# A state-space layer's gate moved from TensorE to VectorE, with the conditioning row turned on chip and one product tile placed in another PSUM bank

## The chip, the cores and the metric

The kernel runs on one core of a Trainium2 chip. The metric is device time in microseconds (us) of one execution, the median of several runs. The engines of the core run their own instruction streams side by side: TensorE (PE: matmuls, and PEld for its weight loads), VectorE (DVE), ScalarE (ACT), GpSimd (POOL), and SyncE (SP), which in this program issues nearly all DMA transfers. Each engine takes its instructions in order, and an instruction that waits for a semaphore holds back all that stands behind it on that engine.

## The reference

The program is a decoder trunk of two layers over 512 tokens of width 1024, float32 throughout. Each layer has a token mixer and a gated feed-forward part with a short convolution; the first layer's mixer is a state-space model (S5), the second's is attention with forgetting. Every one of the four sub-layers is modulated by the conditioning vector c:

```
mod = silu(c) @ ada_w + ada_b
shift, scale, gate = split(mod, 3)
hn = rmsnorm(h) * (1 + scale) + shift
h = h + gate * mixer(hn)
```

The S5 mixer, which is where this case plays, is

```
u = hn @ w_in
y = gelu(state_space(u) + d_skip * u)
y = y * sigmoid(y @ w_glu)
return y @ w_out
```

So for sub-layer 0 three vectors of 1024 numbers are needed from c: shift and scale before u, and the gate only after `y @ w_out`. The next sub-layer (number 1, the feed-forward part) needs its own shift and scale right after that.

## The kernel before, in words

Activations lie with the 1024 channels on the partitions (8 tiles of 128) and the 512 tokens along the free axis. A large product is made tile by tile of 128 output channels. Its weights are split into a rounded part `w_hi` (ScalarE, L280) and the rest `w_lo` (VectorE, L281), its input likewise, and each tile is 8 x 3 matmuls of 128 x 512 into one PSUM bank (`mms`, L297): hi by hi, hi by lo, lo by hi, for each k. A loaded tile of weights is `raw` (L189, 512 KB). There are three buffers for `raw`, five each for `w_hi` and `w_lo`. The eight PSUM banks are two pools of four, `mm` and `aux`.

The stretch around the change runs like this.

1. **Start.** SP loads a first small pack, x, a second pack, and stores `silu(c)` (tile `sc`, 128 x 8) as one row of 1024 numbers in DRAM (`c_row`, L234). It then loads the weights for scale and shift of sub-layer 0 (`in_ada_w`, eight tiles each). TensorE multiplies them (L218) in steps of two tiles, the norm's statistics are made beside it, the columns of 128 numbers are formed by small matmuls (L161, L166) and stored as `ga` and `par` (L171, L174).
2. **S5 loop**, m = 0 to 7. Each turn makes one tile of u (L1169), the group's tables (L957, L973, L980), a scan (L1012, L1023 to L1044), the outputs (L1054, L1062, L1068) and sends y through DRAM. Between these, TensorE does further steps of L218: four for the gate of sub-layer 0 in turns 0 and 1, whose columns follow in turn 1, and eight for shift and scale of sub-layer 1 in turns 2 to 7, the last two turns with two each. The columns of the latter come at the end of the loop.
3. **The head of y @ w_glu.** Four of its eight tiles (HEAD = 4) are accumulated during the loop's end (L1198) in all four banks of `mm`.
4. **The rest of y @ w_glu.** The function `glu` takes a finished tile through a sigmoid (L1256), multiplies it by y (L1257, y read again from DRAM as `yt`) and splits it into `zhi` (L280) and `zlo` (L281). Tiles 4 to 7 are made by `product`, each into a bank of `mm` (L297), so the first of them waits for the sigmoid of tile 0. The residual x is loaded again as `h` (L138) before this.
5. **y @ w_out**, tiles 0 to 7, with `h + gate * tile` on VectorE (L364), followed by the next norm.

In the feed-forward part after it, 56 columns of later shift, scale and gate vectors are made on VectorE instead. One such unit (L248, L249) is a DMA of 128 transposed weight rows (`ada_rows`, 512 KB) and one VectorE instruction that multiplies them by c, broadcast over the partitions (`ada_c`, L240, read from `c_row`), and sums along the row.

Most of the order is set by the framework: it keeps a list in program order, moves instructions ahead by the priorities of its own scheduler, and fixes each engine's order before the run. A stretch at the start is in the order in which it is written (`manual_schedule`). A tile pool that reuses memory makes the new tile wait for the last use of the old.

Of the kernel before, what the change touches and what calls it, by code (L numbers as in the profile page):

```python
# [17 lines left out]
P = 128  # L18
# [28 lines left out]
ROWS_FROM = 1  # L47
# [15 lines left out]
class Trunk:  # L63
# [167 lines left out]
    def spread_c(self):  # L231

        self.cd = self.dram.tile([1, D], F32, name="c_row")
        self.nc.sync.dma_start(self.cd.rearrange("o (k p) -> p (o k)", p=P), self.sc)  # L234

    def ada_pool(self, pool, bufs):

        self.bgpool, self.ada_bufs = pool, bufs
        self.crow = pool.tile([P, D], F32, name="ada_c")
        self.nc.sync.dma_start(self.crow, self.cd.to_broadcast([P, D]))  # L240
# [60 lines left out]
    def product(self, w, ms, nk, x, evac, head=0, tail=0, after=None, ticks=0, halves=HALVES, tail_pool=(), first=None, step=None, apart=False):  # L301
# [17 lines left out]
        for m in ms[head:len(ms) - tail]:  # L319
            wk = self.weights(w[m], nk)  # L320
            ps = self.mm.tile([P, S], F32, name="mmp")
            for c in HALVES if apart else (full,):
                for k in range(nk):
                    self.mms(ps[:, c], wk, x, k, nk, c)
                    if step:
                        step()
            evac(m, ps, full)
            self.tick(ticks)
# [456 lines left out]
class S5(Trunk):  # L785
# [285 lines left out]
    def s5_read_y(self, pool, m):  # L1071
        nc = self.nc
        t = pool.tile([P, L, B], F32, name="yt", bufs=2)
        nc.sync.dma_start(t, self.yd[m].rearrange("g c i b -> (g c) i b"))
        return t[:, ::-1, :]

    def s5(self, i, nxt):
# [5 lines left out]
        with ExitStack() as stack:  # L1083
# [3 lines left out]
            with ExitStack() as start:  # L1087
# [12 lines left out]
                with tc.manual_schedule(engines={ENG.PE, ENG.Activation, ENG.DVE, ENG.SP}):  # L1100
                    self.load_x(self.act)
                    self.load_rest()
                    self.spread_c()
# [52 lines left out]
                    nc.scalar.activation(first, ps.rearrange("p (b j) -> p j b", j=L), AF.Identity, bias=shifted)  # L1156
                    for k in range(2, KT):
                        nc.scalar.activation(x[:, k], x[:, k], AF.Identity, bias=self.par[i][:, k:k + 1])
# [18 lines left out]

            yhi = ylo = None
# [23 lines left out]
            ada = [self.ada_pe(i, (2,), late=True), self.ada_pe(i + 1, (0, 1), late=True)]  # L1202
# [4 lines left out]
            for m in range(KT):  # L1207
                if m:
                    outputs(m - 1)
                with self.behind(*behind):  # L1210
# [6 lines left out]
                    for _ in range((2, 2, 1, 1, 1, 1, 2, 2)[m]):  # L1217
                        next(ada[m >= 2])
                    if m == 1:
                        next(ada[0])  # L1220
# [26 lines left out]
            next(ada[1])  # L1247
        self.load_x(self.ctx.enter_context(tc.tile_pool(name="resid", bufs=1, reuse_waits="tile")))
        with tc.tile_pool(name="s5b", bufs=1, reuse_waits="tile") as pool:
            self.gap(pool, 32, "z_gap")  # L1250
            zhi = pool.tile([P, KT, S], F32R, name="zhi")
            zlo = pool.tile([P, KT, S], F32R, name="zlo")

            def glu(m, ps, cols):
                t = self.tmp.tile([P, S], F32, name="nm_t")
                nc.scalar.activation(t, ps, AF.Sigmoid)  # L1256
                nc.vector.tensor_tensor(tok(t), tok(t), self.s5_read_y(pool, m), ALU.mult)  # L1257
                self.put_parts(zhi[:, m], zlo[:, m], t)

            for m in range(HEAD):  # L1260
                glu(m, gps[m], slice(0, S))
            self.product(self.io["s5_w_glu"], range(HEAD, KT), KT, (yhi, ylo), glu)
            after, y = nxt
            self.product(self.io["s5_w_out"], range(KT), KT, (zhi, zlo), self.add_residual(i), tail=2, after=after)
# [245 lines left out]
def lay_out(inp):  # L1510
# [14 lines left out]
    o["ada_rows"] = np.moveaxis(o["ada_w"][1:], 1, 2).reshape(3, 24, P, D)  # L1525
# [64 lines left out]
```

## Time and profile before

| what | value |
|---|---|
| median of 3 runs | 1240.31 us (1239.1 to 1240.43) |
| the profiled execution, its own time | 1243.44 us |
| its span, first to last instruction | 1241.4 us |
| PE busy | 1213.7 us, 98% |
| PE weight loads busy | 1018.6 us, 82% |
| DVE busy | 899.3 us, 72% |
| ACT busy | 560.5 us, 45% |
| HBM read | 175.57 MB, 147 GB/s over the span |
| S5 loop, in this execution | from about 45 to 204.6 us |
| rest of y @ w_glu | 206.45 to about 228 us |

A busy PE in this profile is not a PE at its peak, since the ends of matmuls are modelled. How long a piece of matmul work takes is better read from the distance of its starts. Times inside a row are counted from the start of the span. A row of the timeline has start, length, engine, line, operation, the tiles written and read, their shape, and a count where several alike are merged; in brackets stands how long the engine was idle before it and what ended that. A row of a window has for each engine its busy time, then the granted TensorE clock (1.00 is full), the busy share of the DMA engines and the GB/s they moved.

### The profile page before, as it was taken

The page shows a single profiled execution, that of the slowest core. Times are in us where ns is not written, and L with a number is a line of the kernel's source. Part 1 is how long each engine was busy: PE and PEld are TensorE (multiplying, and loading weights), DVE is VectorE, ACT ScalarE, POOL GpSimd, SP SyncE. Part 2 cuts the span into 40 slices and gives each one's busy share as a digit, 9 for nine tenths or more (in the row PEclk, how much of TensorE's full clock was granted, in tenths as well). Part 3 has the DMA queues.
Part 4 walks back from the last instruction along what each step waited for, and adds up shares of the span by engine and source line. Part 5 has one row for each costly group of instructions (what it writes and reads, how often), then busy time and mean ns, then how long its engine had stood idle before and what let it go on. Part 6 is the DMA issues. An engine that isn't in the chain of part 4 may idle for free.

```text
span 1241.4 us, 19480 instructions
## 1 busy us (share of the span) xinstructions
PE 1213.7 (98%) x7506; PEld 1018.6 (82%) x7506; DVE 899.3 (72%) x1666; ACT 560.5 (45%) x1031; POOL 56.5 (5%) x109
## 2 busy tenths in 40 slices
PE   6999999999999999999999999999989999999997
PEld 2466678898888788888899888888989999999987
DVE  6898796559887774443567467775799988888865
ACT  3453464334332223333434467654456555555543
POOL 0000000000000000000000134331000000000000
PEclk9899999999999999999999999999999999999999
DMA  9686667326877773222413343330313332333331
GB/s 268 253 275 222 202 196 266 129 100 204 292 267 236 256 248 111 102 75 77 139 69 102 129 142 128 104 130 21 118 52 111 107 117 89 118 105 104 102 86 68
DMA packets 74251, 183.75 MB, mean 148 GB/s; under 512 B 24135, under 2 KB 26527, under 8 KB 73135
## 3 DMA queue, kind: packets, MB, share of 16 engines
q1 hardware_dynamic: 73871, 181.99, 45.2%
q8 instruction: 59, 0.97, 0.3%
q10 hardware_dynamic: 288, 0.52, 0.1%
q14 instruction: 33, 0.27, 0.1%
HBM read 175.57 MB, written 6.92 MB: 147 GB/s over the span
## 4 chain that ended last, share of the span: by engine, by line
PE 83%; DMA 7%; DVE 5%; issue 2%; ACT 1%; POOL 0%; SPq 0%; DVEq 0%; POOLq 0%; ACTq 0%
PE mmp L297 47%; PE mmp L552 10%; DMA ada_raw<-in_ada_rows 5%; PE mmp L1169 5%; PE aux L552 4%; PE mmp L1334 3%; PE aux L973 2%; PE mmp L1198 2%; PE aux L1477 2%; PE mmp L218 1%; PE aux L1460 1%; DVE ada_raw L249 1%; PE aux L1062 1%; PE aux L1054 1%; DVE w_lo L281 1%
## 5 line engine op out<-in xcount | busy, mean ns | idle before, releaser
L280 ACT ACTIVATE w_hi<-raw 128x1024 fp32r<-128x1024 f32 (+4 forms) x197 | 181.2, 927 | 238.8 <-PE mmp L297 150.3
L281 DVE TENSOR_TENSOR w_lo<-raw,w_hi 128x1024 fp32r<-128x1024 f32 (+4 forms) x197 | 210.8, 1071 | 92.5 <-ACT w_hi L280 84.9
L297 PE MATMUL mmp<-a_hi,w_hi 128*128 128x512 f32 (+1 forms) x664 | 242.8, 367 | 2.0 <-ACT a_hi L434 1.3
L297 PE MATMUL mmp<-a_hi,w_lo 128*128 128x512 f32 (+1 forms) x664 | 240.0, 362 | 3.1 <-DVE w_lo L281 3.1
L297 PE MATMUL mmp<-a_lo,w_hi 128*128 128x512 f32 (+1 forms) x664 | 239.7, 362 | 0.0
L297 PE MATMUL mmp<-ghi,w_hi 128*128 128x512 f32 (+1 forms) x394 | 145.2, 369 | 2.1 <-ACT ghi L280 2.1
L297 PE MATMUL mmp<-glo,w_hi 128*128 128x512 f32 (+1 forms) x394 | 145.0, 368 | 0.1
L297 PE MATMUL mmp<-ghi,w_lo 128*128 128x512 f32 (+1 forms) x394 | 144.6, 367 | 0.0
L297 PEld LDWEIGHTS mmp<-a_hi,w_lo 128*128 128x128 f32 x664 | 125.5, 189 | 22.9 <-DVE w_lo L281 3.3
L297 PEld LDWEIGHTS mmp<-a_hi,w_hi 128*128 128x128 f32 x664 | 125.4, 189 | 22.6 <-issue 2.6
L297 PEld LDWEIGHTS mmp<-a_lo,w_hi 128*128 128x128 f32 x664 | 125.7, 189 | 17.5
L249 DVE CUSTOM_DVE_ANT_0 ada_raw<-ada_raw,ada_c,rest 128x1024 f32<-128x1024 f32 x56 | 71.7, 1282 | 29.0 <-DMA ada_raw<-in_ada_rows 28.9
L297 PEld LDWEIGHTS mmp<-ghi,w_hi 128*128 128x128 f32 x394 | 74.3, 189 | 14.3 <-ACT ghi L280 2.6
L297 PEld LDWEIGHTS mmp<-ghi,w_lo 128*128 128x128 f32 x394 | 74.4, 189 | 12.2
L297 PEld LDWEIGHTS mmp<-glo,w_hi 128*128 128x128 f32 x394 | 74.4, 189 | 12.1 <-DVE glo L281 0.5
L364 DVE SCALAR_TENSOR_TENSOR h<-mmp,par,h 128x512 f32<-128x512 f32 (+1 forms) x74 | 49.8, 676 | 42.9 <-PE mmp L297 42.9
L614 ACT ACTIVATE conv<-conv 128x512 f32<-128x512 f32 x44 | 27.6, 631 | 78.5 <-DVE conv L611 78.1
L552 PE MATMUL mmp<-w_lo,w_hi 128*128 128x256 f32 x216 | 59.7, 277 | 0.0
L552 PE MATMUL mmp<-w_hi,w_lo 128*128 128x256 f32 x216 | 59.7, 277 | 0.0
L552 PE MATMUL mmp<-w_hi 128*128 128x256 f32 x216 | 59.7, 277 | 0.0
L1169 PE MATMUL mmp<-a_x,raw 128*128 128x512 f32 x112 | 57.8, 655 | 0.0
L281 DVE TENSOR_TENSOR w_lo<-sums,w_hi 128x1024 fp32r<-128x1024 f32 x40 | 48.5, 1222 | 3.4 <-ACT w_hi L280 2.1
(302 smaller groups left out, 2459.9 us busy)
## 6 DMA issues: line engine op xcount, KB each, us to landing
raw<-in_w_up SPq DMA_DIRECT2D x88, 512.0 KB, 3.3
ada_raw<-in_ada_rows SPq DMA_DIRECT2D x56, 512.0 KB, 4.5
raw<-in_ada_w SPq DMA_DIRECT2D x40, 512.0 KB, 6.4
raw<-in_w_down SPq DMA_DIRECT2D x32, 384.0 KB, 3.1
raw<-in_w_down SPq DMA_DIRECT2D x32, 320.0 KB, 3.0
nf<-nfd SPq DMA_DIRECT2D x8, 1152.0 KB, 5.7
raw<-in_fox_qk SPq DMA_DIRECT2D x16, 512.0 KB, 3.6
h<-in_x SPq DMA_DIRECT2D x8, 512.0 KB, 4.8
```

The lines of the kernel that those rows point to most:

```text
L249: nc.vector.tensor_tensor_reduce(w, w, self.crow, 1.0, self.ada_b[:, i, m:m + 1], ALU.mult, ALU.add, self.par[i][:, m:m + 1])
L280: nc.scalar.activation(hi, src, AF.Copy)
L281: nc.vector.tensor_tensor(lo, src, hi.bitcast(F32), ALU.subtract)
L297: self.last_mm = self.nc.tensor.matmul(o, wt, xt[:, cols], start=(k == 0 and n == 0), stop=(k == nk - 1 and n == 2),)
L364: self.nc.vector.scalar_tensor_tensor(self.h[:, m, cols], ps, self.par[i][:, 16 + m:17 + m], self.h[:, m, cols], op0=ALU.mult, op1=ALU.add,)
L552: self.last_mm = nc.tensor.matmul(o, wt[:, k], xt[:, k], start=(first and k == 0 and n == 0), stop=(k == H - 1 and n == 2), skip_group_che ...
L614: nc.scalar.activation(t, t, AF.Silu)
L973: nc.tensor.matmul(ps[g2][:, j, cols], x[rows, a + j, r].rearrange("p c j -> p (c j)"), self.rr[rows, planes, q, :], start=(j == 0 and r = ...
L1169: nc.tensor.matmul(ps, w[m][:, k, :], x[:, k], start=(k == 0), stop=(k == KT - 1))
L1198: nc.tensor.matmul(gps[m], wt, xt[:, k], start=(k == 0 and part == 0 and xt is yhi), stop=(k == KT - 1 and part == 1))
L1334: self.last_mm = nc.tensor.matmul(ps[q, b][:, :n], xt[:, k, tb], wt, start=(k == 0 and i == 0), stop=(k == KT - 1 and i == 2),)
L1477: nc.tensor.matmul(pv[:, c * P:], self.v[:, hp, k, r].rearrange("p t d -> p (t d)"), pp[:, r, c + 3 * k:NB + 3 * k, :].rearrange("p b t -> ...
```

## The change

It has three parts.

- **The gate of sub-layer 0** is no longer made by TensorE in the S5 loop. It is eight units on VectorE (DMA of `ada_rows` and a row sum each), called by `product` while tiles 5 to 7 of `y @ w_glu` are made, three after a tile (`ticks=3`), with four buffers, and the broadcast of c for them is loaded there too. The steps for shift and scale of sub-layer 1 now come one per turn, m = 0 to 7.
- **The row of c** is turned by TensorE (a transpose to 8 x 128), copied by ScalarE and stored as eight runs of 128 numbers. This stands behind the first tile of u, no longer at the start.
- **Tile 4 of y @ w_glu** goes to a bank of `aux`, its weights are loaded and split ahead of the loop's end, and its matmuls stand ahead of the sigmoids of tiles 0 to 3. Six buffers hold y for the multiplication, where there were two, and the residual is loaded after the product in program order.

```diff
-ROWS_FROM = 1
+ROWS_FROM = 0
...
-        self.cd = self.dram.tile([1, D], F32, name="c_row")
-        self.nc.sync.dma_start(self.cd.rearrange("o (k p) -> p (o k)", p=P), self.sc)
+        nc = self.nc
+        self.cd = self.dram.tile([KT, P], F32, name="c_row")
+        ps = self.aux.tile([KT, P], F32, name="aux")
+        nc.tensor.transpose(ps, self.sc, self.ident)
+        rows = self.tmp.tile([P, S], F32, name="c_rows", tag="ssq", bufs=1)[:KT, :P]
+        nc.scalar.activation(rows, ps, AF.Copy)
+        nc.sync.dma_start(self.cd, rows)
...
-            wk = self.weights(w[m], nk)
-            ps = self.mm.tile([P, S], F32, name="mmp")
+            wk = ready[m] if m in ready else self.weights(w[m], nk)
+            ps = self.aux.tile([P, S], F32, name="aux") if m in ready else self.mm.tile([P, S], F32, name="mmp")
...
-                    self.spread_c()
...
+                    self.spread_c()
                     for k in range(2, KT):
                         nc.scalar.activation(x[:, k], x[:, k], AF.Identity, bias=self.par[i][:, k:k + 1])
...
+            ada = self.ada_pe(i + 1, (0, 1), late=True)
...
-            ada = [self.ada_pe(i, (2,), late=True), self.ada_pe(i + 1, (0, 1), late=True)]
...
-                    for _ in range((2, 2, 1, 1, 1, 1, 2, 2)[m]):
-                        next(ada[m >= 2])
-                    if m == 1:
-                        next(ada[0])
+                    next(ada)
...
-            next(ada[1])
-        self.load_x(self.ctx.enter_context(tc.tile_pool(name="resid", bufs=1, reuse_waits="tile")))
+            next(ada)
+        resid = self.ctx.enter_context(tc.tile_pool(name="resid", bufs=1, reuse_waits="tile"))
...
+            ready = {HEAD: self.weights(self.io["s5_w_glu"][HEAD], KT)}
...
-                nc.vector.tensor_tensor(tok(t), tok(t), self.s5_read_y(pool, m), ALU.mult)
+                nc.vector.tensor_tensor(tok(t), tok(t), self.s5_read_y(pool, m, 6), ALU.mult)
...
-            for m in range(HEAD):
+            self.product(
+                self.io["s5_w_glu"], range(HEAD, HEAD + 1), KT, (yhi, ylo), lambda m, ps, cols: gps.update({m: ps}),
+                ready=ready,
+            )
+            for m in range(HEAD + 1):
                 glu(m, gps[m], slice(0, S))
-            self.product(self.io["s5_w_glu"], range(HEAD, KT), KT, (yhi, ylo), glu)
+            self.ada_pool(pool, 4)
+            self.bg = [self.ada_units(i, [2])]
+            self.product(self.io["s5_w_glu"], range(HEAD + 1, KT), KT, (yhi, ylo), glu, ticks=3)
+            self.load_x(resid)
+            self.done()
...
-    o["ada_rows"] = np.moveaxis(o["ada_w"][1:], 1, 2).reshape(3, 24, P, D)
+    o["ada_rows"] = np.moveaxis(o["ada_w"][0:], 1, 2).reshape(4, 24, P, D)
```

The instruction order shows three places on which the prediction rests. From `y @ w_out` on, the order is the same on every engine.

The first is SP's queue at the start of the program. Before:

```order
L108 DMA first<-in_first 128x168
L138 DMA h<-in_x 128x2x512 x4
L108 DMA rest<-in_rest 128x416
L234 DMA c_row<-sc 128x8x1
L189 DMA raw<-in_ada_w 128x1024 x10
```

And now, up to the store of the row:

```order
L108 DMA first<-in_first 128x168
L138 DMA h<-in_x 128x2x512 x4
L108 DMA rest<-in_rest 128x416
L189 DMA raw<-in_ada_w 128x1024 x10
L189 DMA raw<-in_s_w_in 128x1024
L189 DMA raw<-in_ada_w 128x1024 x6
L800 DMA s_b<-in_s_b 128x1024
L189 DMA raw<-in_s_w_in 128x1024
L1146 DMA s_rr<-in_s_c 128x1024
L1147 DMA s_z<-s_zero 7x8x128
L970 DMA dd<-in_s_dd 128x128
L189 DMA raw<-in_s_w_in 128x1024
```

The row's store (`L239 DMA c_row<-c_rows 8x128`) is the next one. The first weight loads stand directly behind the second pack.

The second is TensorE at the end of the S5 loop, from the last lo products of the head on. Before, with the columns of sub-layer 1 (L161, L166) ahead of tile 4 (L297):

```order
L1198 MATMUL mmp<-a_hi,w_lo 128x512 x4
L161 MATMUL aux<-rest 128x16
L166 MATMUL aux<-sel,ada_rows 128x4 x4
L297 MATMUL mmp<-a_hi,w_hi 128x512
L297 MATMUL mmp<-a_lo,w_hi 128x512
```

Now those columns stand further up, ahead of the last scan's output product (L1067):

```order
L1067 MATMUL aux<-ua,w_1596 128x63 x16
L1204 MATMUL mmp<-a_hi,w_hi 128x512
L1204 MATMUL mmp<-a_lo,w_hi 128x512
L1059 MATMUL aux<-u,t 128x64 x8
L161 MATMUL aux<-rest 128x16
L166 MATMUL aux<-sel,ada_rows 128x4 x4
```

Tile 4 (`L302 MATMUL aux<-a_hi,w_hi 128x512`) follows the last `L1204 MATMUL mmp<-a_hi,w_lo 128x512 x4` directly, in a bank of `aux`.

The third is VectorE during the rest of `y @ w_glu`. Before, from the multiplication of tile 2 and 3 on (`nm_t<-nm_t,yt`), with the weight rests of later tiles (`w_lo`) between:

```order
L1257 TENSOR_TENSOR nm_t<-nm_t,yt 128x8x64 x2
L281 TENSOR_TENSOR w_lo<-raw,w_hi 128x1024
L281 TENSOR_TENSOR zlo<-nm_t,zhi 128x512 x2
L1257 TENSOR_TENSOR nm_t<-nm_t,yt 128x8x64
L281 TENSOR_TENSOR zlo<-nm_t,zhi 128x512
```

Now the same stretch has row sums (`ISA ada_raw`, each followed by a short read of its sum, `ISA par_92`) in between; it is shown from the weight rest of tile 6 up to that of tile 7:

```order
L286 TENSOR_TENSOR w_lo<-raw,w_hi 128x1024
L286 TENSOR_TENSOR zlo<-nm_t,zhi 128x512 x2
L254 ISA ada_raw,par_92<-ada_raw,ada_c,rest 128x1024
L254 ISA par_92 128x1
L1260 TENSOR_TENSOR nm_t<-nm_t,yt 128x8x64 x2
L254 ISA ada_raw,par_92<-ada_raw,ada_c,rest 128x1024
L254 ISA par_92 128x1
L286 TENSOR_TENSOR zlo<-nm_t,zhi 128x512 x2
L254 ISA ada_raw,par_92<-ada_raw,ada_c,rest 128x1024
L254 ISA par_92 128x1
L286 TENSOR_TENSOR w_lo<-raw,w_hi 128x1024
```

Between the weight rest of tile 5 and this stretch stand three more row sums, the multiplications of tiles 0 to 3 and the rests `zlo` of tiles 0 and 1. So six row sums, six multiplications and six `zlo` stand ahead of the weight rest of tile 7, which before stood ahead of the multiplications of tiles 2 and 3.

More of the change, by code (lines that the diff above doesn't have):

```diff
@@ L239, in ada_pool @@
         self.crow = pool.tile([P, D], F32, name="ada_c")
-        self.nc.sync.dma_start(self.crow, self.cd.to_broadcast([P, D]))
+        self.nc.sync.dma_start(self.crow, self.cd.rearrange("k p -> (k p)")[None].to_broadcast([P, D]))
     def ada_units(self, i, thirds):
@@ L299, in mms, with product @@
             )
-    def product(self, w, ms, nk, x, evac, head=0, tail=0, after=None, ticks=0, halves=HALVES, tail_pool=(), first=None, step=None, apart=False):
+    def product(self, w, ms, nk, x, evac, head=0, tail=0, after=None, ticks=0, halves=HALVES, tail_pool=(), first=None, step=None, apart=False, ready=()):
         ms = list(ms)
@@ L1069, in s5_outputs, with s5_read_y @@
         nc.sync.dma_start(self.yd[m].rearrange("g c i b -> (c i) g b"), yg)
-    def s5_read_y(self, pool, m):
+    def s5_read_y(self, pool, m, bufs=2):
         nc = self.nc
-        t = pool.tile([P, L, B], F32, name="yt", bufs=2)
+        t = pool.tile([P, L, B], F32, name="yt", bufs=bufs)
         nc.sync.dma_start(t, self.yd[m].rearrange("g c i b -> (g c) i b"))
```

## The prediction

> **What bounds the kernel now.** I read the page's chain of waits first, then windows of the stretch up to 230 us, its timeline engine by engine, and the groups of the gate product.
>
> ```profile
> PE 83%; DMA 7%; DVE 5%; issue 2%; ACT 1%; POOL 0%; SPq 0%; DVEq 0%; POOLq 0%; ACTq 0%
> ```
>
> The chain is TensorE nearly throughout, but not at the start. In windows of the first 43 us the last two columns are the busy share of the DMA engines and GB/s:
>
> ```profile
> 10.50:16.50 6.00, 4.78 (x14) 1.61 (x12) 4.19 (x37) 2.60 (x5) 0.00 (x0) 1.00 0.91 60
> 16.50:21.00 4.50, 2.69 (x8) 0.36 (x8) 4.34 (x41) 0.00 (x0) 0.00 (x0) 0.75 0.92 235
> ...
> 29.00:43.50 14.50, 14.45 (x71) 5.97 (x70) 11.65 (x26) 2.61 (x5) 0.00 (x0) 1.00 1.03 408
> ```
>
> From 10.5 to 16.5 us the DMA engines are 91% busy and move 60 GB/s; later, equally busy, 408. The transfer that can do this is the row of c, whose 1024 single numbers go out as 4 KB in all:
>
> ```profile
> c_row<-sc SPq DMA_DIRECT2D x1, 4.0 KB, 13.9
> ```
>
> It takes 13.9 us to land. The weights behind it are what TensorE then waits for, up to the last of the scale's products, and the scale itself (L171) after it:
>
> ```profile
> 15.31 0.66 PE L1114 MATMUL aux<-rest,nm_t 128*128 128x128 f32 x4 [0.69 <-ACT nm_t L1111]
> ...
> 24.33 0.28 DVE L876 TENSOR_TENSOR s_pi<-s_w,s_w 128x64 f32<-128x64 f32 x1
> ...
> 28.24 1.05 PE L218 MATMUL mmp<-raw,sc 128*32 128x512 f32 x4 [0.24 <-DMA raw<-in_ada_w]
> ...
> 31.43 0.17 DVE L171 SCALAR_TENSOR_TENSOR ga<-aux,rest 128x8 f32<-128x8 f32 x1 [6.82 <-PE aux L166]
> ```
>
> In the S5 loop the chain is TensorE without a gap worth the name; in the rest of the gate product TensorE runs tile after tile. There the question is whether VectorE, now with slack, keeps it.
>
> **The change part by part.** *The row of c leaves the start.* At 408 GB/s, the rate of the last window, what was not moved from 10.5 to 16.5 us is 6.0 x (408 - 60) = 2.1 MB, 5.1 us. If 16.5 to 21 us is laid to the same transfer, 4.5 x (408 - 235) = 0.8 MB, 1.9 us more: 7.0. The next limits: TensorE is done with the statistics at 16.0 and would find the first weights there, and VectorE reaches the scale's instruction (L171) at 24.6, when L876 ends, in place of 31.43, so 6.8 at most. Behind that TensorE is continuously busy to 43.5 us and the shift's weights come earlier by as much, so what is gained is passed on. I take 6.3, between 5.1 and 6.8: **-6.3**, ends 5.1 and 7.0.
>
> *The turn itself.* A transpose of 8 columns, a copy of 8 x 128 and a DMA of eight runs. Its place is on ScalarE behind the first tile of u and ahead of six biases that TensorE follows. The nearest row:
>
> ```profile
> 31.63 0.18 ACT L174 ACTIVATE par<-aux 128x8 f32<-128x8 f32 x1 [1.69 <-DVE ga L171]
> ```
>
> A copy is about 0.18, and a small product is a quarter of the 0.98 us that four of them take in the next fence; together 0.43. Ends 0 (nothing follows it closely) and 0.6: **+0.3**. SP's queue is held by the store for as long, and behind it stands the store of u's first tile.
>
> *The gate's steps leave the S5 loop.* Pieces of the chain, start and length:
>
> ```profile
> 68.15 1.85 PE mmp L218 x16
> ...
> 86.20 1.85 PE mmp L218 x16
> 88.06 0.32 PE aux L161 x2
> ...
> 89.10 0.98 PE aux L166 x8
> ...
> 90.73 0.69 DVE L1023 TENSOR_TENSOR m<-aux,s_rot 128x512 f32<-128x512 f32 x1 [1.85 <-PE aux L1012]
> ```
>
> Sixteen of these records are two steps, 1.85 us. Turns 0 and 1 had four steps and the columns (0.32 + 0.98), and keep two steps: 1.85 + 1.30 = 3.15 us of TensorE less. VectorE waits there 1.85 us for the scan's input, which would go; beyond it VectorE is near its own limit:
>
> ```profile
> 57.00:92.00 35.00, 34.92 (x295) 22.16 (x295) 30.14 (x47) 17.36 (x59) 0.00 (x0) 1.00 0.83 264
> ```
>
> The third entry after the length is VectorE, 30.1 of 35 us. I take the 1.85 and 0.55, less than half of the remaining 1.3: **-2.4**, ends 0 and 3.15.
>
> *The loop's end.* The last two turns lose two steps (1.85) and take in the columns of sub-layer 1 (1.30), which stood behind the loop. But here VectorE sets the pace:
>
> ```profile
> 157.00:176.00 19.00, 19.00 (x218) 12.52 (x212) 17.99 (x28) 11.50 (x28) 0.00 (x0) 1.00 0.72 224
> ...
> 185.30 0.73 DVE L1044 TENSOR_TENSOR ua<-ua,ub 128x512 f32<-128x512 f32 x1
> ...
> 187.53 2.00 PE L1062 MATMUL aux<-ua,w 64*128 64x63 f32 x32
> ```
>
> The last scan is ready at 186.0, TensorE takes it at 187.5 after fillers, so 1.5 us are open. A wait is added as well: L171 now stands between the last scan and its `ua`, and waits for the columns; behind it are `ua`, y's last tile and, on TensorE, the second half of the head. **-0.6**, the difference of 1.85 and 1.30; ends -1.9 and +1.3.
>
> *Tile 4 in another bank.*
>
> ```profile
> 203.65 1.08 PE L1198 MATMUL mmp<-a_hi,w_lo 128*128 128x512 f32 x4
> 204.56 0.29 PE L161 MATMUL aux<-rest 128*128 128x16 f32 x2
> ...
> 206.45 0.53 PE L297 MATMUL mmp<-a_hi,w_hi 128*128 128x512 f32 x1 [0.72 <-ACT nm_t L1256]
> ```
>
> Tile 4 began 1.9 us after the head's last product, 1.2 for the columns and 0.72 for the sigmoid. Now it follows at once, if its weights are split by then. SP's order has their load ahead of y's last read, and VectorE has room before that read's split:
>
> ```profile
> 193.24 1.29 SPq L1074 DMA_DIRECT2D yt<-s_yd  x3
> ...
> 198.13 1.17 DVE L1187 TENSOR_TENSOR a_lo<-yt,a_hi 128x512 fp32r<-128x512 f32 x1 [5.56 <-ACT a_hi L1186]
> ```
>
> So **-1.9**; ends -1.9 and 0, if they come late.
>
> *Eight row sums on VectorE.* Distances of starts, not lengths, are what counts for a full queue:
>
> ```profile
> 204.13 1.23 DVE L281 TENSOR_TENSOR w_lo<-raw,w_hi 128x1024 fp32r<-128x1024 f32 x1 [2.25 <-PE mmp L1198]
> ...
> 206.99 2.40 DVE L1257 TENSOR_TENSOR nm_t<-nm_t,yt 128x512 f32<-128x512 f32 x2
> 209.26 1.25 DVE L281 TENSOR_TENSOR w_lo<-raw,w_hi 128x1024 fp32r<-128x1024 f32 x1
> 210.39 1.32 DVE L281 TENSOR_TENSOR zlo<-nm_t,zhi 128x512 fp32r<-128x512 f32 x2
> 211.59 1.25 DVE L281 TENSOR_TENSOR w_lo<-raw,w_hi 128x1024 fp32r<-128x1024 f32 x1
> ...
> 244.99 0.75 DVE L364 SCALAR_TENSOR_TENSOR h<-mmp,par,h 128x512 f32<-128x512 f32 x1 [2.75 <-PE mmp L297]
> ...
> 250.43 0.75 DVE L364 SCALAR_TENSOR_TENSOR h<-mmp,par,h 128x512 f32<-128x512 f32 x1 [2.75 <-PE mmp L297]
> ...
> 292.88 1.28 DVE L249 CUSTOM_DVE_ANT_0 ada_raw<-ada_raw,ada_c,rest 128x1024 f32<-128x1024 f32 x1
> 294.08 0.08 DVE L249 DVE_READ_ACCUMULATOR2_ANT par<- 128x1 f32 x1
> ```
>
> A weight rest costs 1.13, a multiplication 1.135, a `zlo` 0.60, a row sum 1.20; a tile of 24 matmuls 5.44. The weight rest of tile 5 cannot start before 204.13: its buffer is read by the head's last lo product. In the new order the rest of tile 7 ends after that one, six row sums, six multiplications, the rest of tile 6, six `zlo` and itself: 1.13 + 7.2 + 6.8 + 1.13 + 3.6 + 1.23 = 21.1, at 225.2. TensorE begins tile 7 at 204.56 + 3 x 5.44 = 220.9 and needs that rest with its third matmul, at 221.3. It waits **3.9 us**, and nothing hides it. The rest of tile 6 is just in time (215.8 against 215.9), and of w_out's tile 0 also (230.5 against 230.7); the gate and the residual are there before tile 0 of w_out ends. Ends: 2 (the sigmoids and row loads fit better than I stack them) and 5 (each hand-over from ScalarE costs a little).
>
> **The sum:** -6.3 + 0.3 - 2.4 - 0.6 - 1.9 + 3.9 = -7.0. Made against the profiled execution (span 1241.4, own time 1243.44) that gives 1236.4; this execution lay 3.1 above the median, so from the median of 1240.31 it is **1233.3**. The cover of the new DMA and of the row sums is the stretch of the gate product:
>
> ```profile
> 204.50:228.30 23.80, 23.08 (x107) 19.18 (x107) 19.69 (x22) 14.39 (x21) 0.00 (x0) 1.00 0.66 212
> ```
>
> The DMA of the rows and of the broadcast, nine times 512 KB, falls into room: 66% busy. VectorE was busy for 19.7 of 23.8 us, and six row sums are 7.2. If that cover were gone, each late row would push the weight rest of tile 7.
>
> **The rivals.** *The wait in tile 7 also costs the clock.* Shortly before 47 us TensorE has only small products (L161, L166, L1150), and then the granted clock, the column ahead of the DMA share, is half:
>
> ```profile
> 46.00:48.00 2.00, 2.00 (x8) 1.48 (x9) 2.00 (x3) 0.91 (x4) 0.00 (x0) 0.52 0.00 0
> ...
> 50.00:52.00 2.00, 2.00 (x3) 0.67 (x2) 1.90 (x5) 2.00 (x4) 0.00 (x0) 0.50 0.93 346
> ...
> 47.05 9.96 PE mmp L1169 x16
> ...
> 58.95 3.63 PE mmp L1169 x8
> ...
> 284.00:286.00 2.00, 0.72 (x5) 0.52 (x4) 2.00 (x6) 0.12 (x1) 0.00 (x0) 1.00 0.75 250
> ```
>
> A tile of 16 records took 9.96 in place of 2 x 3.63, so 2.7 us went to half the clock. After 3.9 us of waiting the same can happen: 1236.0. Against it: TensorE idled for 1.3 of 2 us from 284 us on and kept the full clock. [...]
>
> *No wait in tile 7:* VectorE's stretch is looser than stacked and TensorE sees none of it. 1233.3 - 3.9 = 1229.4. For it, the end of 2 above; against it, a plain sum of durations.
>
> *The start's gain is not passed on:* the loads were late for another reason (buffers, the second pack), or VectorE's parameter work becomes the bound. Then 1239.6, no difference. Against it stands the 91% busy at 60 GB/s.
>
> *Slower:* the queue cannot bring the rows. From 193.2 us SP's order has 7.3 MB up to tile 7's weights (eight reads of y of 256 KB, the broadcast, three weight tiles and six rows of 512 KB). They must be there by 223, when ScalarE has to round them: 245 GB/s. Below 186 GB/s the wait grows by more than the 9.5 us that turn -7.0 into +2.5. At the 127 GB/s of the slowest stretch nearby,
>
> ```profile
> 43.50:57.00 13.50, 13.23 (x43) 7.15 (x42) 10.80 (x22) 8.59 (x18) 0.00 (x0) 0.75 0.40 127
> ```
>
> it would be 57.5 us, 27.7 more: 1261. Against it: that stretch was not asked for more, its DMA share is 0.40, and the start moved 408.
>
> **How the numbers follow.** Forecast 0.45, clock 0.22, no wait 0.13, start not passed on 0.13, slower 0.07. The forecast's own range is 1229.5 to 1237.5. To leave out no more than 2 in 10 I take 1229.0 to 1238.5. About 0.2%, 2.5 us, is what can be told from no change here. Faster: the first three, 0.80; same 0.13; slower 0.07.
>
> **What would show it.** L171 of the start near 25 us and no window at 60 GB/s; the S5 loop's last head product some 9 us earlier; tile 4 right behind it; one idle time of about 4 us in tile 7, put down to `w_lo`; the granted clock after it. If L171 stays near 31 us, or tile 7 waits 10 us for a DMA, the prediction is wrong.

## The result and the profile after

The changed kernel takes 1237.47 us in the median of 20 runs (1233.91 to 1239.93), against 1240.57 us for the kernel before (1238.62 to 1247.93). The ratio is 0.9962, with a 95% interval of 0.9949 to 0.9975: about 4.7 us faster, between 3.1 and 6.3. The two medians lie only 3.1 us apart, at the weak end of that interval, and the means of the same runs 4.6. A second set of 12 runs beside three experiments gave 0.9968 (0.9954 to 0.9983). The profiled execution took 1237.85 us, its span 1236.0 us.

The start, in windows of the changed kernel (length, the five engines, granted clock, DMA share, GB/s), and the scale's instruction on VectorE:

```profile
10.50:16.50 6.00, 5.31 (x14) 1.81 (x14) 3.64 (x30) 3.24 (x6) 0.00 (x0) 1.00 1.02 408
16.50:21.00 4.50, 4.21 (x32) 1.01 (x29) 4.06 (x41) 0.00 (x0) 0.00 (x0) 1.00 1.02 401
...
25.34 0.16 DVE L171 SCALAR_TENSOR_TENSOR ga<-aux,rest 128x8 f32<-128x8 f32 x1
```

The stretch at 60 GB/s is gone, and the scale is there at 25.34 in place of 31.43. The next rows are TensorE at the first S5 head (so the first product of the tables, L978, is called here; L973 in the kernel before), then at the end of the head of the gate product and the start of tile 4:

```profile
40.24 8.73 PE L1174 MATMUL mmp<-a_x,raw 128*128 128x512 f32 x16
48.90 2.02 PE L978 MATMUL aux<-s_rr,x 64*128 64x80 f32 x32
...
193.35 1.07 PE L1204 MATMUL mmp<-a_hi,w_lo 128*128 128x512 f32 x4
194.25 0.39 PE L302 MATMUL aux<-a_hi,w_hi 128*128 128x512 f32 x1
```

The first head starts at 48.90. In the kernel before it was

```profile
56.93 2.02 PE L973 MATMUL aux<-s_rr,x 64*128 64x80 f32 x32
```

Tile 4 follows the head's last product at 194.25 without a gap, 12.2 us earlier than before. Then TensorE runs into the wait in tile 7:

```profile
211.05 0.40 PE L302 MATMUL mmp<-a_lo,w_hi 128*128 128x512 f32 x1
214.91 0.79 PE L302 MATMUL mmp<-a_hi,w_lo 128*128 128x512 f32 x1 [3.46 <-DVE w_lo L286]
215.50 0.63 PE L302 MATMUL mmp<-a_hi,w_hi 128*128 128x512 f32 x1
...
218.06 0.45 PE L302 MATMUL mmp<-a_hi,w_hi 128*128 128x512 f32 x1
218.35 0.40 PE L302 MATMUL mmp<-a_lo,w_hi 128*128 128x512 f32 x1
```

It is idle for 3.46 us ahead of the third matmul, until the weight rest comes from VectorE, and then the products start 0.43 us apart instead of 0.23 until 218.1: half clock. On VectorE the queue between the weight rest of tile 5 and that of tile 7 is without a hole (first and last of its rows):

```profile
194.14 1.23 DVE L286 TENSOR_TENSOR w_lo<-raw,w_hi 128x1024 fp32r<-128x1024 f32 x1 [4.82 <-ACT w_hi L285]
195.28 1.28 DVE L254 CUSTOM_DVE_ANT_0 ada_raw<-ada_raw,ada_c,rest 128x1024 f32<-128x1024 f32 x1
...
212.41 1.30 DVE L254 CUSTOM_DVE_ANT_0 ada_raw<-ada_raw,ada_c,rest 128x1024 f32<-128x1024 f32 x1
213.62 0.10 DVE L254 DVE_READ_ACCUMULATOR2_ANT par<- 128x1 f32 x1
213.62 1.24 DVE L286 TENSOR_TENSOR w_lo<-raw,w_hi 128x1024 fp32r<-128x1024 f32 x1
```

Five places of TensorE's timeline, in us from the span's start, the changed kernel in two profiled executions (the second beside the experiments):

| place | before | changed | changed, second |
|---|---|---|---|
| first head of the S5 loop | 56.93 | 48.90 (-8.0) | 48.11 (-8.8) |
| end of the head of y @ w_glu | 204.73 | 194.42 (-10.3) | 193.63 (-11.1) |
| first product of y @ w_out | 228.41 | 221.57 (-6.8) | 222.14 (-6.3) |
| first product of the feed-forward part | 274.72 | 267.81 (-6.9) | 268.40 (-6.3) |
| TensorE's end | 1233.76 | 1228.10 (-5.7) | 1224.28 (-9.5) |

All of the gain is in the first line. Between the first head and the feed-forward part, where parts one and three of the change lie, the changed kernel takes 218.91 and 220.29 us, the kernel before 217.79. Behind that the instructions are the same, and the difference still moves by 1 to 3 us.

### The profile page after: what moved, and what is told of

Same layout as the page of the kernel before. It is cut to its first block, busy times and chain, and to the rows that moved or that the text cites. A ratio compares the mean times of both kernels' runs of the same rounds, so it can differ in the third digit from the quotient of the medians.

```text
span 1236.0 us, 19402 instructions
## 1 busy us (share of the span) xinstructions
PE 1207.5 (98%) x7465; PEld 1018.8 (82%) x7465; DVE 907.2 (73%) x1682; ACT 560.9 (45%) x1030; POOL 57.4 (5%) x109
## 4 chain that ended last, share of the span: by engine, by line
PE 82%; DVE 7%; DMA 7%; issue 2%; ACT 1%; SPq 0%; DVEq 0%; ACTq 0%
PE mmp L302 47%; PE mmp L557 10%; DMA ada_raw<-in_ada_rows 5%; PE aux L557 4%; PE mmp L1174 4%; PE mmp L1345 3%; PE aux L978 2%; PE aux L1488 2%; PE aux L1471 1%; DVE ada_raw L254 1%; DVE w_lo L286 1%; PE aux L1067 1%; PE aux L1059 1%; PE mmp L218 1%; PE aux L1441 1%
## 5 line engine op out<-in xcount | busy, mean ns | idle before, releaser
L302 PE MATMUL mmp<-a_hi,w_lo 128*128 128x512 f32 (+1 forms) x656 | 238.7, 364 | 6.5 <-DVE w_lo L286 6.5
L302 PE MATMUL mmp<-a_hi,w_hi 128*128 128x512 f32 (+1 forms) x656 | 241.2, 369 | 1.4 <-ACT a_hi L439 1.4
L302 PE MATMUL mmp<-a_lo,w_hi 128*128 128x512 f32 (+1 forms) x656 | 237.9, 363 | 0.0
L302 PEld LDWEIGHTS mmp<-a_hi,w_lo 128*128 128x128 f32 x656 | 125.5, 192 | 26.7 <-DVE w_lo L286 7.5
L302 PE MATMUL mmp<-ghi,w_hi 128*128 128x512 f32 (+1 forms) x394 | 145.0, 368 | 1.5 <-ACT ghi L285 1.5
L302 PE MATMUL mmp<-glo,w_hi 128*128 128x512 f32 (+1 forms) x394 | 144.8, 367 | 0.2 <-DVE glo L286 0.2
L302 PE MATMUL mmp<-ghi,w_lo 128*128 128x512 f32 (+1 forms) x394 | 144.6, 367 | 0.0
L302 PEld LDWEIGHTS mmp<-a_hi,w_hi 128*128 128x128 f32 x656 | 125.3, 192 | 21.9 <-issue 2.6
L302 PEld LDWEIGHTS mmp<-a_lo,w_hi 128*128 128x128 f32 x656 | 125.7, 192 | 17.5
L254 DVE CUSTOM_DVE_ANT_0 ada_raw<-ada_raw,ada_c,rest 128x1024 f32<-128x1024 f32 x64 | 82.0, 1282 | 27.8 <-DMA ada_raw<-in_ada_rows 27.8
L302 PEld LDWEIGHTS mmp<-ghi,w_hi 128*128 128x128 f32 x394 | 74.4, 189 | 13.7 <-ACT ghi L285 1.9
L302 PEld LDWEIGHTS mmp<-glo,w_hi 128*128 128x128 f32 x394 | 74.3, 189 | 12.3 <-DVE glo L286 0.5
L302 PEld LDWEIGHTS mmp<-ghi,w_lo 128*128 128x128 f32 x394 | 74.4, 189 | 12.2
L1174 PE MATMUL mmp<-a_x,raw 128*128 128x512 f32 x112 | 54.7, 626 | 0.0
```

The lines of the kernel that those rows point to most:

```text
L254: nc.vector.tensor_tensor_reduce(w, w, self.crow, 1.0, self.ada_b[:, i, m:m + 1], ALU.mult, ALU.add, self.par[i][:, m:m + 1])
L302: self.last_mm = self.nc.tensor.matmul(o, wt, xt[:, cols], start=(k == 0 and n == 0), stop=(k == nk - 1 and n == 2),)
L1174: nc.tensor.matmul(ps, w[m][:, k, :], x[:, k], start=(k == 0), stop=(k == KT - 1))
```

## The experiments

### Which part of the change pays

Four kernels on one chip. The first is the kernel before with only the row of c changed: the new `spread_c` of the change's diff, with its line in `ada_pool`, called behind the first tile of u.

```
+        nc.tensor.transpose(ps, self.sc, self.ident)
...
+        nc.sync.dma_start(self.cd, rows)
```

The second keeps the old `spread_c` with its 1024 pieces and moves only the call:

```
                     self.load_rest()
-                    self.spread_c()
...
                     nc.scalar.activation(first, ps.rearrange("p (b j) -> p j b", j=L), AF.Identity, bias=shifted)
+                    self.spread_c()
```

The third is the changed kernel with the old `spread_c` called at the start again:

```
                     self.load_rest()
+                    self.spread_c()
...
-                    self.spread_c()
```

The fourth is the changed kernel with the gate back on TensorE and no row sums:

```
+                    for _ in range((2, 2, 1, 1, 1, 1, 2, 2)[m]):
+                        next(ada[m >= 2])
...
-            self.ada_pool(pool, 4)
-            self.bg = [self.ada_units(i, [2])]
```

The row of c alone:

> The kernel before, with the row of c alone changed: turned by TensorE and stored in eight runs behind the first tile of u. My theory: the scattered store held the weights at the start, and the whole gain is passed on, as TensorE is busy behind it: 6.0 us by the prediction's two first terms, 8.0 us by the place of the first head of the S5 loop in the two traces (56.93 against 48.90 us). So 0.9935 to 0.995 of before. Rival, the start's gain is not passed on: 1.000. Rival, part of the 8.0 us is the granted clock, which happened to be half for a shorter time in one profiled execution (46 to 52.7 us against 41 to 45): then nearer 0.995, and the two ends of the half clock lie as far apart as before.

Its place alone:

> The kernel before, with the store of the row of c as it was, 1024 pieces of 4 bytes, but issued where the changed kernel issues it, behind the first tile of u. No transpose, no copy. If only the place matters (the DMA engines have room there, share 0.40 from 43.5 to 57 us, and nobody waits), it gains as much as the turned row: 0.994 to 0.995. If the pieces hold whatever stands behind them wherever they are, about 14 us of landing now stall the store of u's first tile and the weights of the S5 loop: TensorE waits up to 8 to 14 us there, and the time is 1.000 to 1.006 of before.

The row of c undone:

> The changed kernel with the row of c put back as it was before: scattered, at the start. Parts one and three are left. If the parts add up as the two traces have them (turns 0 and 1 of the S5 loop -2.8, the loop's end +0.5, tile 4 -1.9, tile 7's wait and half clock +5.4), it is 1.2 us slower than before: 1.001. By the prediction's terms it is -2.4 - 0.6 - 1.9 + 3.9 = -1.0: 0.999. If the start's gain is not passed on in the changed kernel, it is as fast as that, 0.996.

The gate on TensorE:

> The changed kernel with the gate of sub-layer 0 put back on TensorE, in turns 0 and 1 of the S5 loop; no row sums in the gate product. Parts two and three are left. My theory: the row sums cost more (wait in tile 7 3.6 and half clock behind it 1.7) than they save (2.8 in the loop, less 0.5 at its end), so this is about 3 us faster than the changed kernel: 8.0 + 1.9 us below before, 0.992. Rival, the row sums pay: 0.996 or more. In its trace tile 7 has no idle time ahead of its third matmul.

| kernel | median us | ratio to before | interval |
|---|---|---|---|
| row of c alone | 1234.91 | 0.9958 | 0.9937 to 0.9978 |
| its place alone | 1235.85 | 0.9968 | 0.9953 to 0.9982 |
| changed, row of c undone | 1242.77 | 1.0019 | 1.0002 to 1.0037 |
| changed, gate on TensorE | 1234.48 | 0.9955 | 0.9937 to 0.9972 |

The row of c alone gives what the whole change gives. Without it, the other two parts are slower than before, by 2.4 us (0.2 to 4.6). In the eleven profiles of kernels in which the store does not stand at the start, the first S5 head begins 7.4 to 8.8 us earlier than before; where it stands there, 0.1 later. These are the heads with the row of c alone, with its place alone, and with the row of c undone:

```profile
48.22 2.02 PE L978 MATMUL aux<-s_rr,x 64*128 64x80 f32 x32
...
48.78 2.02 PE L973 MATMUL aux<-s_rr,x 64*128 64x80 f32 x32
...
57.02 2.02 PE L973 MATMUL aux<-s_rr,x 64*128 64x80 f32 x32
```

The times of the first two kernels show less than that, 5.2 and 4.0 us. In their profiled executions the rest is lost in the S5 loop, up to the end of the head of the gate product: 155.1 and 150.9 us against 147.8 before. The first has long stretches at half clock there (the last section); in the second TensorE waits 1.5 us for the last part of y, with 3.4 us at half clock behind it. Whether other executions lose it in the same way is not shown.

The place is enough. The 1024 pieces, issued at 28.6 us in SP's order, still take 13.9 us to land (the last entry, after the size). They stand behind loads that move 420 GB/s up to 34 us, and from 36 us on, while they land, the DMA engines are asked for next to nothing else. TensorE's start is the same: the first head 8.2 us earlier.

```profile
c_row<-sc SPq DMA_DIRECT2D x1, 4.0 KB, 13.9
...
L234 SPq DMA_DIRECT2D c_row<-sc x1: 392/392/392, 28.6 to 28.6; - x1
...
32.00:34.00 2.00, 2.00 (x11) 0.43 (x10) 1.86 (x5) 0.00 (x0) 0.00 (x0) 1.00 1.05 420
34.00:36.00 2.00, 2.00 (x8) 0.56 (x11) 1.93 (x4) 0.00 (x0) 0.00 (x0) 1.00 0.84 215
36.00:38.00 2.00, 2.00 (x11) 0.68 (x4) 1.83 (x9) 1.14 (x3) 0.00 (x0) 1.00 0.05 6
```

The packets in the traces show what the pieces do at the start, and it is not their own length. In the kernel before they leave the queue between 8.5 and 10 us, 9 ns each. The packets of 4096 bytes that follow, the first weights, then take long: from 10.5 to 14.5 us 37 of them begin, with a median of 1.85 us each. In the changed kernel 396 begin in that time, at 0.16 us each. So it is the weights behind the pieces that are held; what holds them, once the pieces have left, the traces don't show.

Whether the turn adds anything to the move can't be told: 0.9958 and 0.9968 lie within each other's intervals.

With the gate on TensorE the expected 3 us are not shown by the times: 0.9955 against 0.9962 and 0.9968, with intervals of 0.0013 to 0.0018 to each side. Its trace has the direction. The profile shows no wait of TensorE between 190 and 240 us, and from the first head to the feed-forward part it takes 216.68 us, 2.2 and 3.6 less than the changed kernel.

### The wait in tile 7 and the clock behind it

Four kernels on another chip: the changed kernel again as the base, and it with three edits. The row sums spread out:

```
-            self.product(self.io["s5_w_glu"], range(HEAD + 1, KT), KT, (yhi, ylo), glu, ticks=3)
+            self.product(self.io["s5_w_glu"], range(HEAD + 1, KT), KT, (yhi, ylo), glu, ticks=1)
             self.load_x(resid)
-            self.done()
             after, y = nxt
-            self.product(self.io["s5_w_out"], range(KT), KT, (zhi, zlo), self.add_residual(i), tail=2, after=after)
+            self.product(self.io["s5_w_out"], range(KT), KT, (zhi, zlo), self.add_residual(i), tail=2, after=after, ticks=1)
+            self.done()
```

TensorE kept busy in the wait (`fill` is 15 in tile 7, and 0 elsewhere):

```
         for n, (wt, xt) in enumerate(((hi, xhi), (hi, xlo), (lo, xhi))):
+            if n == 2 and k == 0 and fill:
+                spare = self.aux.tile([P, S], F32, name="aux")
+                for _ in range(fill):
+                    self.nc.tensor.matmul(spare, hi, xhi[:, cols], start=True, stop=True)
```

Tile 4 back in the head's bank:

```
-            ready = {HEAD: self.weights(self.io["s5_w_glu"][HEAD], KT)}
...
-            self.product(
-                self.io["s5_w_glu"], range(HEAD, HEAD + 1), KT, (yhi, ylo), lambda m, ps, cols: gps.update({m: ps}),
-                ready=ready,
-            )
-            for m in range(HEAD + 1):
+            for m in range(HEAD):
                 glu(m, gps[m], slice(0, S))
+            self.product(self.io["s5_w_glu"], range(HEAD, HEAD + 1), KT, (yhi, ylo), glu)
```

The base:

> The changed kernel itself, as the base for the three runs beside it on one chip. 0.996 of before, with half-clock stretches in places that differ from run to run.

The row sums spread out:

> The changed kernel with one row sum instead of three behind each of tiles 5, 6 and 7 of the gate product, and one behind each of the first tiles of the output product, each ahead of the tile whose gate it is. My theory: VectorE's queue ahead of the weight rest of tile 7 is 4.8 us of row sums shorter, that rest is ready before TensorE needs it, and both the wait (3.6) and the half clock behind it (1.7) go: 5.3 us below the changed kernel, 0.992 of before. Rival one, only the wait goes and the clock falls somewhere else: 3.6. Rival two, the row sums between the output product's evictions delay the weight rests there, and the wait comes back a few tiles later: no better than the changed kernel.

The wait filled:

> The changed kernel with 15 more products of 128 x 512 ahead of the third matmul of tile 7, into a bank that is free and read by nobody: 15 x 0.227 = 3.4 us of TensorE work in the place of its wait for the weight rest. The rest comes as late as before. If it is the idle time that halves the clock behind it, the matmuls from the third on take 0.23 us each at once, and 1.7 us are saved: 0.9985 of the changed kernel, and the granted clock in that stretch is 1. If the half clock there has another cause (it comes with the stretch), the first six matmuls behind still take 0.43 each, and nothing is saved or up to 0.3 lost.

Tile 4 in the head's bank:

> The changed kernel with tile 4 back in the bank that the head's first tile leaves, its weights loaded behind the head's sigmoids in program order. The gap ahead of tile 4 comes back, 0.7 to 1.0 us. If tile 7's start is set by VectorE's queue, which is full from tile 5's weight rest on and does not see this, tile 7 waits that much less and the time is the changed kernel's (within 0.5 us): the third part of the change is worth nothing beside the row sums. If TensorE sets it, 0.7 to 1.0 us slower. If the later load of tile 4's weights pushes VectorE's queue back as well, 2 us slower or more.

| kernel | median us | ratio to before | interval |
|---|---|---|---|
| changed, again | 1235.82 | 0.9968 | 0.9954 to 0.9983 |
| row sums spread | 1231.40 | 0.9927 | 0.9906 to 0.9949 |
| wait filled | 1234.94 | 0.9963 | 0.9947 to 0.9978 |
| tile 4 in the head's bank | 1234.04 | 0.9949 | 0.9933 to 0.9966 |

**Spread row sums.** TensorE's waits from 190 to 240 us, of the changed kernel and then of this one (us in total, times, longest):

```profile
PE mmp L302 <- DVE w_lo L286: 3.5, 1, 3.5
```

```profile
PE mmp L302 <- DVE zlo L286: 0.6, 1, 0.6
PE mmp L302 <- ACT zhi L285: 0.3, 1, 0.3
```

The wait for the weight rest is gone, and 0.9 us of small ones are there at the first tile of the output product. From the end of the head to the first product of the output it takes 21.60 us (194.10 to 215.70), four tiles of 5.4, where the changed kernel took 27.15 and 28.51. By the ratios the time falls by 0.0041, 5.1 us, and the two intervals do not overlap. Nothing of the wait came back between the evictions of the output product; its first tile alone makes the output product 1.5 us longer (47.77 against 46.24).

**The wait filled.** First the base, then the filled kernel, TensorE in the same place:

```profile
214.45 0.80 PE L302 MATMUL mmp<-a_hi,w_lo 128*128 128x512 f32 x1 [3.46 <-DVE w_lo L286]
215.04 0.63 PE L302 MATMUL mmp<-a_hi,w_hi 128*128 128x512 f32 x1
215.47 0.63 PE L302 MATMUL mmp<-a_lo,w_hi 128*128 128x512 f32 x1
...
216.00:220.00 4.00, 4.00 (x11) 3.17 (x10) 3.54 (x6) 1.02 (x2) 0.00 (x0) 0.50 0.32 113
```

```profile
211.87 3.59 PE L305 MATMUL aux<-a_hi,w_hi 128*128 128x512 f32 x15
215.48 0.50 PE L306 MATMUL mmp<-a_hi,w_lo 128*128 128x512 f32 x1
215.82 0.39 PE L306 MATMUL mmp<-a_hi,w_hi 128*128 128x512 f32 x1
216.05 0.40 PE L306 MATMUL mmp<-a_lo,w_hi 128*128 128x512 f32 x1
...
216.00:220.00 4.00, 4.00 (x19) 3.27 (x19) 4.00 (x7) 2.75 (x3) 0.00 (x0) 1.00 0.69 254
```

The fillers take 3.6 us, the weight rest comes no earlier, and the matmuls behind start 0.23 apart: 19 instead of 11 in the same 4 us, at a granted clock of 1.00 instead of 0.50. So the idle time is what costs the clock here, as far as one filled execution can show it: all three profiled executions that wait 3.5 us at this place have the half clock. The granted clock of the runs agrees: its mean is 0.9938 over the 12 runs of the filled kernel and 0.9922 over 32 of the changed one, 0.0016 more (standard error 0.0007); 3.4 us at half clock in a span of 1235 us are 0.0014. From the end of the head to the first product of the output this kernel takes 25.61 us, 1.5 and 2.9 less than the changed kernel's two executions. The times can't tell so little: 0.9963 against 0.9968.

**Tile 4 in the head's bank.** Its waits:

```profile
PE mmp L302 <- DVE w_lo L286: 1.8, 1, 1.8
PE mmp L302 <- ACT nm_t L1258: 1.6, 1, 1.6
```

The wait for the sigmoid is back with 1.6 us, and the wait in tile 7 is shorter by the same 1.6: 3.5 in sum, as in the changed kernel. In this execution the shorter wait was followed by the half clock as well:

```profile
214.97 0.50 PE L302 MATMUL mmp<-a_hi,w_lo 128*128 128x512 f32 x1 [1.84 <-DVE w_lo L286]
...
216.00:218.00 2.00, 2.00 (x6) 1.57 (x5) 2.00 (x4) 0.83 (x2) 0.00 (x0) 0.50 0.86 295
```

From the end of the head to the first product of the output it takes 27.25 us, against 27.15. So beside these row sums the other bank is worth nothing. VectorE's queue sets when tile 7 goes on, and what TensorE gains ahead of it, it waits for there. By the ratio the kernel is not slower than its base (0.9949 and 0.9968, intervals overlap).

### Is it the place of the row sums or the length of the queue?

```
-            self.product(self.io["s5_w_glu"], range(HEAD + 1, KT), KT, (yhi, ylo), glu, ticks=3)
+            self.product(self.io["s5_w_glu"], range(HEAD + 1, KT), KT, (yhi, ylo), glu, ticks=2)
             self.load_x(resid)
+            self.tick(2)
             self.done()
```

The second kernel is the one with spread row sums, but with none behind tile 7, and the spread one ran again beside them.

```
-            self.product(self.io["s5_w_glu"], range(HEAD + 1, KT), KT, (yhi, ylo), glu, ticks=1)
+            self.product(self.io["s5_w_glu"], range(HEAD + 1, KT - 1), KT, (yhi, ylo), glu, ticks=1)
+            self.product(self.io["s5_w_glu"], range(KT - 1, KT), KT, (yhi, ylo), glu)
```

Two behind each tile:

> The changed kernel with two row sums instead of three behind each of tiles 5, 6 and 7, and the last two ahead of the output product. VectorE's order then has two row sums and two of the zlo fewer ahead of tile 7's weight rest, 2 x 1.2 + 2 x 0.6 = 3.6 us, and all of them behind it, ahead of the weight rest of the output product's first tile. My theory, that the queue is one sum and TensorE waits where its next weight rest stands: no wait in tile 7 (0 to 0.3 us), but the rest of the output product's first tile comes some 10 us behind that of tile 7, at about 221.4, and TensorE, 5.4 us earlier there, waits 4 to 5 us for it: as slow as the changed kernel, 0.996. Rival, each row sum taken from ahead of tile 7 is a gain and what is behind fits beside the output product: 3.5 to 5 us below it, 0.992 to 0.993.

None behind tile 7:

> The kernel with one row sum behind each tile, but none behind tile 7: the one that stood ahead of tile 7's zlo there, for which TensorE waited 0.6 us, moves behind the output product's first tile. If that wait goes and nothing takes its place, 0.3 to 0.9 us below the kernel with one behind each tile. If the row sums now bunch ahead of the next weight rests or evictions of the output product, TensorE waits there instead: no better, or 1 us worse.

The spread one again:

> The kernel with one row sum behind each tile again, beside the two others and for a narrower interval: 0.9927 of before as in its first run; if that was luck of the half-clock stretches, up to 0.996.

| kernel | median us | ratio to before | interval |
|---|---|---|---|
| two behind each of tiles 5 to 7 | 1236.36 | 0.9970 | 0.9949 to 0.9991 |
| spread, none behind tile 7 | 1233.03 | 0.9936 | 0.9912 to 0.9961 |
| spread, again | 1231.60 | 0.9933 | 0.9907 to 0.9959 |

With two behind each tile, tile 7 has no wait, and the first tile of the output product has two:

```profile
217.88 0.50 PE L302 MATMUL mmp<-zhi,w_hi 128*128 128x512 f32 x1 [1.63 <-ACT w_hi L285]
...
220.79 0.50 PE L302 MATMUL mmp<-zhi,w_lo 128*128 128x512 f32 x1 [2.17 <-DVE w_lo L286]
```

The second wait is for a weight rest of VectorE. The first is for rounded weights, which ScalarE makes behind a `zhi` that waited for VectorE's multiplication:

```profile
215.65 0.63 ACT L285 ACTIVATE zhi<-nm_t 128x512 fp32r<-128x512 f32 x1 [3.43 <-DVE nm_t L1260]
```

Together the two are 3.8 us, where 4 to 5 were expected, and the time is the changed kernel's. Two row sums less ahead of one weight rest helped nothing here, since they then stood ahead of the next: 3.8 us of waits in place of 3.5. From the first S5 head to the feed-forward part this kernel takes 219.44 us, the spread ones 214.86, 215.12 and 215.10. Leaving out the row sum behind tile 7 changes nothing: TensorE still waits 0.6 us for `zlo` and 0.6 for `zhi`, so that row sum was not what it waited for.

The spread kernel, at 0.9927 and 0.9933, beats both kernels of the case. It is some 8 to 9 us faster than before.

## Why the prediction came out as it did

The forecast was 1233.3, -7.0 us; the ratio gives -4.7 (-3.1 to -6.3). The direction and the mechanisms are there, and the size is a third less by the ratio and more than half less by the medians. Against the profile, at the first product of the output, the sum is nearly met (-6.8 and -6.3), but that is luck: the terms were off and cancelled, as the table has it. Part of it may also belong to the one profiled execution of the kernel before, which lay 2.9 us above the median of that kernel.

| terms of the prediction | predicted | changed | changed, second |
|---|---|---|---|
| start and turn of c (-6.3 + 0.3) | -6.0 | -8.0 | -8.8 |
| S5 loop and its end (-2.4 - 0.6) | -3.0 | -2.3 | -2.3 |
| tile 4 and tile 7 (-1.9 + 3.9) | +2.0 | +3.5 | +4.8 |
| sum | -7.0 | -6.8 | -6.3 |

**The start** was right in its mechanism and place: L171 at 25.34 for "near 25 us", 6.1 us earlier. Most of what came on top is the half clock that the kernel before had from 46.1 to 52.9 us. In the changed kernel the tile of 16 products took 8.73 in place of 9.96 there, with half clock from 40.7 to 44.1 us, and 7.19 in the second execution, with none. The prediction quoted that stretch, but took it as unchanged. The rival "not passed on" falls: eleven profiles have the gain at the first head, and undoing this part loses it, in the times 7.1 us between the ratios 0.9962 and 1.0019. The row's store was the right cause; the busy DMA engines, though, which the prediction laid to the row's pieces, were busy with the slow weights behind them. Its term for the turn, 0.3 us, is too small to be seen in any run.

**The loop** was sized 0.7 too high. With the gate on TensorE, from the first head to the end of the head of the gate product, it takes 147.66 us without a half clock; in the eight profiles with the row sums that have no half clock there either, it takes 145.49 to 145.53 (145.98 in the ninth, which has one). So taking the gate out is worth 2.1 to 2.2, the columns moved in included. The wait of L171 for the columns, for which the range had up to +1.3, came and cost TensorE nothing that the trace shows:

```profile
174.62 0.17 DVE L171 SCALAR_TENSOR_TENSOR ga<-aux,rest 128x8 f32<-128x8 f32 x1 [4.17 <-PE aux L166]
174.70 0.68 DVE L1046 TENSOR_TENSOR ua<-m,s_rot 128x512 f32<-128x512 f32 x1
```

VectorE stands still for 4.2 us with `ua` behind it, while TensorE has products of the head in store and no gap there.

**Tile 4 and tile 7.** The gap ahead of tile 4 is gone as predicted, and the wait in tile 7 measured 3.46 of the predicted 3.9, with VectorE's queue filled as counted. The step that failed is that nothing was set down for the clock behind the wait: that was a rival with 0.22, at 2.7 us. It happened in both profiles of the changed kernel, for 7 and for 12 products at 0.43 us in place of 0.23, which is 1.5 and 2.5 us, and it was not there when the wait was filled. On the line of the table the wait and the clock leave 0.4 and 0.7 us without a place. The rival's time, 1236.0, is what the ratio gives (1240.57 x 0.9962 = 1235.9), partly by luck, since the start gained 2.0 to 2.8 more than either counted. By the traces' records of the granted clock, the 45 stretches of half clock up to 1222 us in the thirteen profiles have three lengths: 36 take 3.41 us, eight take 6.83 and one 10.24. In tile 7 the first execution of the changed kernel has one from 214.77 to 218.18 us, 3.41 long, which began 3.3 us into the wait; in the second, the windows from 212 to 220 us give 6.8. The 7 and the 12 slow products lie inside them. Why the same kernel has one length in one execution and twice that in the other is not shown.

What the prediction held against this rival, that 1.3 us of idle time had kept the full clock in the kernel before, was too weak an argument. That wait, 1.29 to 1.36 us long, stands in all thirteen profiles, and in seven of them the clock is half within 1 us behind it. At the same wait the changed kernel had full clock in one execution and half in the other: from the first product of the feed-forward part to its second stage it took 125.36 us in the first, 123.90 in the second, and 123.90 before.

The two other rivals: no wait in tile 7 is ruled out by the 3.46 us. The DMA queue brought the rows in time, since the wait ended with `w_lo` and VectorE's queue had no hole.

The weight of the terms was also seen wrongly. Part three's 1.9 us has two halves: 1.2 for the columns, which went to the loop with part one, and 0.7 for the bank, which tile 7's wait gives back in full, as the experiment shows. Parts one and three together cost time, and what they cost is paid out of the gain at the start.

## What to carry to other kernels

In these runs a row of VectorE's order was a queue with appointments. A row sum put into it cost TensorE nothing until the first weight rest behind it was late (3.46 us in tile 7), and what TensorE gained ahead of that point it waited away: without the 1.6 us for the sigmoid ahead of tile 4, the wait in tile 7 was 1.6 us longer. One piece ahead of each appointment was right in this kernel (0.9927 and 0.9933 of before), and three (0.9962 and 0.9968) or two (0.9970) were not; moving the same lot past one appointment made the next one late, by 3.8 us in two waits. A store of many tiny pieces belongs where no load that somebody waits for is queued behind it: the same 13.9 us cost the first S5 head 7.4 to 8.8 us at the start and nothing 25 us later.

## What the runs showed of the hardware that was not expected

**The half clock also comes without an idle time.** In the profiled execution of the kernel with the row of c alone, the profile shows no wait of TensorE from 76 to 94 us, and the granted clock is half for some 10 us:

```profile
80.00:84.00 4.00, 4.00 (x52) 3.75 (x48) 2.80 (x4) 0.26 (x2) 0.00 (x0) 0.96 0.96 334
84.00:88.00 4.00, 4.00 (x12) 2.33 (x11) 3.74 (x7) 1.95 (x7) 0.00 (x0) 0.50 0.91 297
88.00:92.00 4.00, 4.00 (x12) 2.82 (x12) 0.00 (x0) 2.57 (x11) 0.00 (x0) 0.50 0.07 26
92.00:94.00 2.00, 2.00 (x6) 0.50 (x7) 0.00 (x0) 0.00 (x0) 0.00 (x0) 0.52 0.00 0
```

A second such stretch begins at 108 us. From the first head to the end of the head of the gate product this execution took 155.1 us, against 147.7 with neither. In the trace of the kernel before, such a stretch stands at 145 to 148.5 us, and at the same place in that of the changed kernel with the row of c undone; nine of the thirteen profiles have none in this loop. What starts it in the S5 loop, whose products are small, was not tried.

**The same wait costs the clock in one execution and not in another.** A wait of 3.1 us for a weight rest stands between 912 and 931 us in all thirteen profiles. Behind it the clock is half in nine of them and full in four. The changed kernel has both, here in its second execution and then in its first:

```profile
917.62 0.39 PE L302 MATMUL mmp<-a_hi,w_lo 128*128 128x256 f32 x1 [3.12 <-DVE w_lo L286]
...
918.00:922.00 4.00, 4.00 (x38) 4.00 (x37) 4.00 (x5) 0.64 (x1) 0.00 (x0) 1.00 0.69 213
```

```profile
918.91 0.58 PE L302 MATMUL mmp<-a_hi,w_lo 128*128 128x256 f32 x1 [3.08 <-DVE w_lo L286]
...
918.00:922.00 4.00, 3.09 (x14) 3.09 (x15) 4.00 (x4) 0.21 (x1) 0.00 (x0) 0.50 0.40 131
```

So with seven in thirteen behind 1.3 us and nine in thirteen behind 3.1, the length of a wait alone does not decide it in these profiles.

**Most of the spread of one kernel goes with it.** Over the 221 runs of this study (each with its time and mean granted clock), the time within a kernel moves by 1.1 us for 0.001 of mean clock, and the clock accounts for three quarters of the variance. The spread kernel's two profiled executions have spans of 1228.2 us at 0.996 and 1232.5 at 0.991. A difference of 2 us between two profiles of this kernel says nothing by itself; a stage cut between two fixed places of TensorE's timeline does, as the 145.49 to 145.53 above.
